# One core, two layers of FFN, mixer and FFN: products on the raw residual, LayerNorm applied when they leave PSUM

## The chip, the core and the metric

The kernel runs on one core of a Trainium2 chip, in one launch. The metric is the time on the device in microseconds. A core has TensorE (PE) for matmuls, VectorE (DVE) and ScalarE (ACT) for elementwise work, GpSimd (POOL), and DMA queues, here all fed by SyncE (SP). The engines run side by side, each through its own list of instructions in order, and wait for each other by semaphores.

## What is computed

Two layers over 384 tokens, 128 of context and 256 latent, of width 1024. Each layer is a gated FFN, a mixer (latent attention beside a bidirectional RG-LRU behind one input projection) and a second gated FFN. Each sub-layer's input is the normalised residual, scaled and shifted by modulation vectors that differ between the two kinds of token:

```
def trunk_layer(x, mod, mixer, lp):
    m = [mod[:, k, None, :] for k in range(N_MOD)]
    h = x * (1 + m[1]) + m[0]
    x = layer_norm(ALPHA * x + 0.5 * m[2] * swiglu(h, lp["w_ffn_up"][0], lp["w_ffn_down"][0]),
                   lp["ln_g"][0], lp["ln_b"][0])
    h = x * (1 + m[4]) + m[3]
    y, aux = mixer(h)
    x = layer_norm(ALPHA * x + m[5] * y, lp["ln_g"][1], lp["ln_b"][1])
    h = x * (1 + m[7]) + m[6]
    x = layer_norm(ALPHA * x + 0.5 * m[8] * swiglu(h, lp["w_ffn_up"][1], lp["w_ffn_down"][1]),
                   lp["ln_g"][2], lp["ln_b"][2])
    return x, aux

def swiglu(h, w_up, w_down):
    u = jnp.einsum("btd,df->btf", h, w_up)
    return jnp.einsum("btf,fd->btd", jax.nn.silu(u[..., :D_FF]) * u[..., D_FF:], w_down)
```

The modulation is silu(cond) @ w_mod + b_mod, nine vectors of 1024 per layer. D_FF is 2816.

## The kernel before

The residual X lies in SBUF with features on the partitions, as KD = 8 chunks of 128 features by T = 384 tokens; COND are the two token ranges, 0 to 128 and 128 to 384. Every product runs as three matmuls: weights and inputs are each split into a high and a low part, and `mm3` (lines 319 to 322) adds wh·xh, wh·xl and wl·xh. `piece` (line 306) makes the weight parts: ScalarE casts wh (line 315), VectorE subtracts for wl (line 316), both put ahead in the order by a priority. Three buffers hold split weights, four PSUM tiles hold accumulators. `hh` and `hl` are the two parts of a sub-layer's input. A scheduler lays the instructions of each engine in one order at build time, so what stands behind a waiting instruction waits too.

An FFN (`ffn`, line 466) has 22 pairs of products, gate and value, each of 8 chunks, so 48 matmuls a pair. `gated` (line 472) takes a pair out of PSUM: silu on ScalarE, a product on VectorE (line 475), a cast on ScalarE, a subtraction on VectorE (line 477). The down products follow, and `Residual.add` (line 347) adds each finished chunk into X (line 351). GpSimd sums X and its squares over the chunks (lines 360 and 361).

At each of the five boundaries between sub-layers `next_input` (line 453) runs: some modulation steps, then `boundary_vectors`, then `moments` (line 378: mean and deviation per token, by small matmuls against a constant), then `normalise` (line 394), which subtracts the mean and multiplies by the reciprocal deviation chunk by chunk on VectorE (lines 400 and 401), out of PSUM tiles in which both are broadcast over the partitions. `split_affine` (line 275) turns each chunk into hh and hl: on ScalarE, with VectorE taking half of the chunks' h (line 284) and all subtractions (line 286). GpSimd scales X for the residual (line 461). Products of the next sub-layer can start when the first chunk is through.

The mixer (line 536) projects with 14 products: four for the convolution and the RG-LRU (`conv` reads PSUM directly), two for the KV latent, one for the rotary key, three for the query, four for the gate branch. GpSimd turns the rotary key's weights (lines 608 and 609) and takes the power for the KV norm (line 335). The output product w_o goes two columns blocks at a time, one after the other.

Between all this `Pump` makes the modulation vectors from 18 MB of weights each layer, a step at a time: a step of `by_vector` is eight VectorE instructions of 512 columns (lines 250 and 252), a step of `by_tensor` goes over TensorE (line 238). The tables say where:

```
PUMPED = (by_vector((0, 2), (0, 3), (0, 4)) + by_tensor((0, 5)) + by_tensor((0, 6), (0, 7)) + by_tensor((0, 8), (1, 0))
          + by_vector((1, 1), (1, 3), (1, 4)) + by_tensor((1, 2)) + by_tensor((1, 5), (1, 6)) + by_tensor((1, 7), (1, 8)))
UP = [f for f in range(3, 21) if f % 3]
PLAN = ((UP, ()), (UP, ()), ((), ()), ((), ()))
NEXT_STEPS = (3, 3, 4, 3, 3)
MIX_STEPS = (14, 10)
```

So there are twelve vector steps in FFN (0,0) and twelve in FFN (0,1), three or four tensor steps at each boundary, 14 and 10 in the mixers.

## Time and profile before

| | |
|---|---|
| median of 3 runs | 1605.43 us (1602.26 to 1608.64) |
| the profiled execution | 1607.12 us, of which the profile's span is 1605.3 us |
| busy share of the span | PE 97%, DVE 59%, ACT 41%, POOL 10% |
| matmul instructions | 9234 |
| end of FFN (0,0) and start of mixer 0 | 315 us |
| mixer 0 to FFN (0,1) | 510 to 545 us |
| FFN (0,1) to FFN (1,0) | 809 to 832 us |
| FFN (1,0) to mixer 1 | 1096 us |
| mixer 1 to FFN (1,1) | 1294 to 1325 us |

Times in the rows are microseconds from the span's start. An engine's busy time is the sum of its instructions' records; a matmul's record is longer than the distance to the next one's start, because they are pipelined. "<-" behind a row's idle time names what released the engine. In names, a number behind the tile is left out.

### The profile page before, as it was taken

How to read it: one execution, taken by the hardware profiler on the slowest of the kernel's cores; microseconds unless marked ns; L12 is line 12 of the kernel's file. 1: busy time of each engine (PE TensorE's matmuls, PEld its weight loads, DVE VectorE, ACT ScalarE, POOL GpSimd, SP SyncE). 2: the span in 40 equal slices, each digit the busy share in tenths (PEclk: the TensorE clock that was granted, in tenths of full speed). 3: DMA queues.
4: the chain of work that ended last, by engine and by line, in shares of the span. 5: the costliest groups of instructions: out<-in, count | busy, mean ns of one | idle time of the engine just before them, and what ended most of it. 6: DMA issues, size and time to landing. Idle time of an engine off the chain costs nothing.

```text
span 1605.3 us, 22927 instructions
## 1 busy us (share of the span) xinstructions
PE 1552.4 (97%) x9234; PEld 1448.7 (90%) x9234; DVE 949.3 (59%) x1568; ACT 660.5 (41%) x1068; POOL 161.0 (10%) x142
## 2 busy tenths in 40 slices
PE   6999999999999999999999999999999989999997
PEld 5899999987668899999989999997867789999996
DVE  3778754477986946863474444345788664444334
ACT  3533323268743533332253333234775444333321
POOL 0000002220004100001220000032000240000011
PEclk9999999999999999999999999999999989999998
DMA  8866563346644535563454343334565214433331
GB/s 295 278 215 203 173 202 133 116 151 209 226 166 157 184 117 199 184 203 119 134 183 150 106 137 119 128 107 157 152 193 197 79 53 131 142 121 128 121 118 40
DMA packets 214790, 249.93 MB, mean 156 GB/s; under 512 B 26394, under 2 KB 193308, under 8 KB 211612
## 3 DMA queue, kind: packets, MB, share of 16 engines
q1 hardware_dynamic: 214684, 248.47, 46.6%
q8 instruction: 72, 1.18, 0.3%
q14 instruction: 34, 0.28, 0.1%
HBM read 245.52 MB, written 1.88 MB: 154 GB/s over the span
## 4 chain that ended last, share of the span: by engine, by line
PE 87%; DVE 5%; issue 3%; DMA 2%; ACT 2%; POOL 1%; SPq 0%; DVEq 0%; POOLq 0%; ACTq 0%
PE acc L320 26%; PE acc L321 26%; PE acc L322 26%; PE gm L238 2%; DVE wl L316 1%; PE acc L753 1%; DMA wm<-in_w_mod_dram 1%; PE ms L375 1%; PE pv L786 1%; DMA ws<-in_w_ffn_up_dram 1%; PE ms L769 1%; ACT wh L315 0%; DVE hl L286 0%; POOL sum_f L361 0%; PE ms L320 0%
## 5 line engine op out<-in xcount | busy, mean ns | idle before, releaser
L315 ACT CAST wh<-ws 128x1024 fp32r<-128x1024 f32 (+1 forms) x332 | 336.2, 1014 | 779.4 <-PE acc L321 545.3
L316 DVE TENSOR_TENSOR wl<-ws,wh 128x1024 fp32r<-128x1024 f32 (+1 forms) x332 | 411.3, 1240 | 382.3 <-ACT wh L315 380.7
L320 PE MATMUL acc<-hh,wh 128*128 128x384 f32 x1280 | 428.6, 339 | 7.9 <-ACT hh L278 7.4
L322 PE MATMUL acc<-hh,wl 128*128 128x384 f32 x1280 | 431.0, 337 | 2.9 <-DVE wl L316 2.9
L321 PE MATMUL acc<-hl,wh 128*128 128x384 f32 x1280 | 431.1, 338 | 1.1 <-DVE hl L286 1.0
L320 PEld LDWEIGHTS acc<-hh,wh 128*128 128x128 f32 x1280 | 241.8, 190 | 15.7 <-ACT hh L278 9.2
L322 PEld LDWEIGHTS acc<-hh,wl 128*128 128x128 f32 x1280 | 241.9, 189 | 8.6 <-DVE wl L316 5.5
L321 PEld LDWEIGHTS acc<-hl,wh 128*128 128x128 f32 x1280 | 241.9, 189 | 8.5 <-DVE hl L286 4.9
L320 PE MATMUL acc<-gh,wh 128*128 128x384 f32 x704 | 236.9, 336 | 0.0
L321 PE MATMUL acc<-gl,wh 128*128 128x384 f32 x704 | 236.4, 336 | 0.0
L322 PE MATMUL acc<-gh,wl 128*128 128x384 f32 x704 | 236.1, 335 | 0.0
L320 PEld LDWEIGHTS acc<-gh,wh 128*128 128x128 f32 x704 | 132.2, 188 | 0.4 <-issue 0.4
L321 PEld LDWEIGHTS acc<-gl,wh 128*128 128x128 f32 x704 | 132.4, 188 | 0.0
L322 PEld LDWEIGHTS acc<-gh,wl 128*128 128x128 f32 x704 | 132.2, 188 | 0.0
L475 DVE TENSOR_TENSOR a<-a,acc 128x384 f32<-128x384 f32 x87 | 48.1, 553 | 123.1 <-PE acc L322 121.4
L252 DVE SCALAR_TENSOR_TENSOR gsum<-wm,sil,gsum 128x512 f32<-128x512 f32 x168 | 120.2, 764 | 0.0
L320 PE MATMUL acc<-hh_in,wh 128*128 128x384 f32 x336 | 111.6, 337 | 5.9 <-ACT hh_in L278 5.9
L321 PE MATMUL acc<-hl_in,wh 128*128 128x384 f32 x336 | 113.9, 339 | 0.0
L322 PE MATMUL acc<-hh_in,wl 128*128 128x384 f32 x336 | 113.9, 339 | 0.0
L360 POOL TENSOR_TENSOR sum_f<-X 128x384 f32<-128x384 f32 x4 | 5.1, 1281 | 841.2 <-DVE X L351 841.2
L320 PEld LDWEIGHTS acc<-hh_in,wh 128*128 128x128 f32 x336 | 62.7, 188 | 7.8 <-ACT hh_in L278 6.8
L238 PE MATMUL gm<-wm,sil 128*32 128x128 f32 (+2 forms) x640 | 62.2, 428 | 3.3 <-DVE G L915 1.2
(268 smaller groups left out, 1750.4 us busy)
## 6 DMA issues: line engine op xcount, KB each, us to landing
ws<-in_w_ffn_up_dram SPq DMA_DIRECT2D x84, 1024.0 KB, 5.1
wm<-in_w_mod_dram SPq DMA_DIRECT2D x56, 1024.0 KB, 6.6
ws<-in_w_ffn_down_dram SPq DMA_DIRECT2D x32, 1024.0 KB, 5.3
wm<-in_w_mod_dram SPq DMA_DIRECT2D x32, 512.0 KB, 4.5
ws<-in_w_ffn_down_dram SPq DMA_DIRECT2D x16, 768.0 KB, 4.5
ws<-in_w_in_dram SPq DMA_DIRECT2D x12, 1024.0 KB, 5.3
...
```

Source lines behind the costliest of these rows:

```text
L238: nc.tensor.matmul(self.ps[32 * g : 32 * g + 32, :n], lhsT, wv[:, g], start=self.fresh, stop=stop)
L252: nc.vector.scalar_tensor_tensor(self.sum[:, r], wv[:, kk], s, self.sum[:, r], op0=ALU.mult, op1=ALU.add)
L315: nc.scalar.copy(parts[0], src)
L316: nc.vector.tensor_tensor(parts[1], src, parts[0].bitcast(F32), op=ALU.subtract)
L320: nc.tensor.matmul(ps, wh, xh, start=start, stop=False)
L321: nc.tensor.matmul(ps, wh, xl, start=False, stop=False)
L322: nc.tensor.matmul(ps, wl, xh, start=False, stop=stop)
L375: nc.tensor.matmul(self.pt[:, 2 * i + j : 2 * i + j + 1], src[:, i * P : (i + 1) * P], mean_w[:, 0:1], start=False, stop=stop and i == T / ...
L475: nc.vector.tensor_tensor(a, a, px[:, :T], op=ALU.mult)
L753: nc.tensor.matmul(views[i], qT[hf][0:96, h % 4, q0 : q0 + P], kT[hf][0:96, h % 4, k0:k1], start=True, stop=True)
L769: nc.tensor.transpose(t0[:, (2 * j + i) * P : (2 * j + i + 1) * P], pr_[:, (0, 512)[i] + j * P : (0, 512)[i] + (j + 1) * P], ident)
L786: nc.tensor.matmul(o[:, P:T], v, pTs[e][:, (j - 1) * 256 : j * 256], start=(j == 1), stop=(j == 3))
```

## The change

The new `hh` and `hl` are wider: EXT = T + 4 columns. In the first 384 columns of chunk c stands G·X, with G = (1 + scale)·ln_g per feature and kind of token, split into high and low part by `split_raw` as soon as X of that chunk is final; nothing of the mean is taken off. `extend` puts -G of the two kinds of token and then B of both (B = (1 + scale)·ln_b + shift) into the four extra columns. A product over all 388 columns gives W·G·X, -W·G and W·B. `settle` takes it out of PSUM: it copies the four columns, adds mean · (-W·G) to the product by token range, and multiplies by the reciprocal deviation; the last two columns are handed on as a bias. `stats` (the small matmuls and the power) and `broadcasts` (mean and deviation over all partitions, copied by ScalarE to SBUF as stat tiles) run between the first products of the next sub-layer. `carry` then brings X itself to its normalised and scaled form on GpSimd, three instructions a chunk, where VectorE did two and GpSimd one before.

In the mixer all 14 products go through `settled`, and their readers take the bias in separate instructions for the two token ranges; conv's first product is held until mean and deviation are there. In w_o the last two blocks run together over the chunks, and the other chunks are split before their residuals are added. The step tables move: the boundaries have none, the mixers 20 and 16, FFN (0,1) four, and FFN (1,0) twelve, four of them on TensorE and eight on VectorE.

```diff
-          + by_vector((1, 1), (1, 3), (1, 4)) + by_tensor((1, 2)) + by_tensor((1, 5), (1, 6)) + by_tensor((1, 7), (1, 8)))
+          + by_vector((1, 1)) + by_tensor((1, 2)) + by_vector((1, 3), (1, 4)) + by_tensor((1, 5), (1, 6)) + by_tensor((1, 7), (1, 8)))
-PLAN = ((UP, ()), (UP, ()), ((), ()), ((), ()))
-NEXT_STEPS = (3, 3, 4, 3, 3)
-MIX_STEPS = (14, 10)
+PLAN = ((UP, ()), (UP[:4], ()), (UP, ()), ((), ()))
+MIX_STEPS = (20, 16)
+EXT = T + 4
...
+    def split_raw(c, G):
+        h32 = tmp.tile([P, T], F32, tag="t1", bufs=3, name=f"raw_{n_ps[0]}_{c}")
+        for r, (t0, t1) in enumerate(COND):
+            nc.scalar.activation(hh[:, c, t0:t1], X[:, c, t0:t1], AF.Copy, scale=G[:, c, r : r + 1])
+            nc.vector.tensor_scalar_mul(h32[:, t0:t1], X[:, c, t0:t1], G[:, c, r : r + 1])
+        nc.vector.tensor_tensor(hl[:, c, :T], h32, hh[:, c, :T].bitcast(F32), op=ALU.subtract)
...
+        def extend(self):
+            for o, v, sign in ((T, self.G, -1.0), (T + 2, self.B, 1.0)):
+                nc.scalar.mul(hh[:, :, o : o + 2], v, sign)
+                nc.vector.scalar_tensor_tensor(hl[:, :, o : o + 2], v, sign, hh[:, :, o : o + 2].bitcast(F32),
+                                               op0=ALU.mult, op1=ALU.subtract)
+        def broadcasts(self):
...
+            self.mean, self.rstd = (tmp.tile([P, T], F32, tag=f"sum{i}", name=f"stat{i}_{name}", bufs=1) for i in range(2))
+            nc.scalar.copy(self.mean, pm[:, :T])
+            nc.scalar.copy(self.rstd, pr[:, :T])
+        def carry(self):
             for c in range(KD):
-                nc.vector.tensor_tensor(X[:, c, :], X[:, c, :], pm[:, :T], op=ALU.subtract)
-                nc.vector.tensor_tensor(X[:, c, :], X[:, c, :], pr[:, :T], op=ALU.mult)
-                yield c
+                nc.gpsimd.tensor_tensor(X[:, c, :], X[:, c, :], self.mean, op=ALU.subtract)
+                nc.gpsimd.tensor_tensor(X[:, c, :], X[:, c, :], self.rstd, op=ALU.mult)
+                nc.gpsimd.tensor_scalar(X[:, c, :], X[:, c, :], self.ag[:, 0, c : c + 1], self.ag[:, 1, c : c + 1],
+                                        op0=ALU.mult, op1=ALU.add)
+        def settle(self, dst, ps, name):
+            v = tmp.tile([P, 4], F32, tag="ext", name=f"ext_{name}")
+            nc.vector.tensor_copy(v, ps[:, T:EXT])
+            for r, (t0, t1) in enumerate(COND):
+                nc.vector.scalar_tensor_tensor(dst[:, t0:t1], self.mean[:, t0:t1], v[:, r : r + 1], ps[:, t0:t1],
+                                               op0=ALU.mult, op1=ALU.add)
+            nc.vector.tensor_tensor(dst, dst, self.rstd, op=ALU.mult)
+            return v[:, 2:4]
...
-    def next_input(res, l, s, nl, nm, steps):
-        pump.step(steps)
-        pump.finish()
-        G, B, ag = boundary_vectors(l, s, nl, nm)
-        hh, hl = h_tiles(f"{nl}{nm}")
-        for c in res.normalise():
-            split_affine(hh, hl, c, G, B)
-        for c in range(KD):
-            nc.gpsimd.tensor_scalar(X[:, c, :], X[:, c, :], ag[:, 0, c : c + 1], ag[:, 1, c : c + 1],
-                                    op0=ALU.mult, op1=ALU.add)
-        return hh, hl
...
+                    bg = raw.settle(a, pg, f"g{l}{s}{f}")
+                    by = raw.settle(y, px, f"y{l}{s}{f}")
+                    for r, (t0, t1) in enumerate(COND):
+                        nc.scalar.activation(a[:, t0:t1], a[:, t0:t1], AF.Silu, bias=bg[:, r : r + 1])
+                        nc.vector.scalar_tensor_tensor(a[:, t0:t1], y[:, t0:t1], by[:, r : r + 1], a[:, t0:t1],
+                                                       op0=ALU.add, op1=ALU.mult)
...
-                    product(pg[:, :T], wg, i * P, hh, hl)
-                    product(px[:, :T], wx, i * P, hh, hl)
-                    gated(f, pg, px)
+                    product(pg, wg, i * P, width)
+                    if prev is not None and f == 0:
+                        prev.stats()
+                    product(px, wx, i * P, width)
+                    if prev is not None and f == 0:
+                        prev.broadcasts()
+                    gated(f, pg, px, prev)
+                    if prev is not None and f == 0:
+                        prev.carry()
```

What this does to the order on the engines, at three places. First VectorE (DVE) at the boundary from FFN (0,0) to mixer 0; `wl` are low parts of weights, `h` and `hl` the input, `ms` the broadcast mean and deviation, `m_f` the variance. Before:

```order
L351 SCALAR_TENSOR_TENSOR X<-acc_2655,gate_2125,X 128x128
L351 SCALAR_TENSOR_TENSOR X<-acc_2655,gate_2125,X 128x256
L316 TENSOR_TENSOR wl_3072<-ws_3068,wh_3071 128x1024
L400 TENSOR_TENSOR X<-X,ms_2832 128x384
L389 SCALAR_TENSOR_TENSOR m_f_2883<-ms_2824,m_f_2883 128x3
L400 TENSOR_TENSOR X<-X,ms_2832 128x384 x5
L401 TENSOR_TENSOR X<-X,ms_2888 128x384 x2
L284 TENSOR_SCALAR h_66_0_2894<-X,G_2866,B_2867 128x128
L284 TENSOR_SCALAR h_66_0_2894<-X,G_2866,B_2867 128x256
L401 TENSOR_TENSOR X<-X,ms_2888 128x384
L286 TENSOR_TENSOR hl_2875<-h_66_0_2894,hh_2874 128x384
```

and in the changed kernel, where `raw_7` is chunk 7 times G and `ext` the four columns:

```order
L360 SCALAR_TENSOR_TENSOR X<-acc_2696,gate_2122,X 128x128
L360 SCALAR_TENSOR_TENSOR X<-acc_2696,gate_2122,X 128x256
L291 TENSOR_SCALAR raw_7_2873<-X,G_2124 128x128
L291 TENSOR_SCALAR raw_7_2873<-X,G_2124 128x256
L322 TENSOR_TENSOR wl_3040<-ws_3036,wh_3039 128x1024
L292 TENSOR_TENSOR hl<-raw_7_2873,hh 128x384
L429 COPY ext_0ux_3007<-acc_2918 128x4
L322 TENSOR_TENSOR wl_3084<-ws_3036,wh_3083 128x1024
L394 SCALAR_TENSOR_TENSOR m_f_2961<-ms_2947,m_f_2961 128x3
L429 COPY ext_0ux_3022<-acc_2966 128x4
L322 TENSOR_TENSOR wl_3164<-ws_3160,wh_3163 128x1024
L431 SCALAR_TENSOR_TENSOR s0ux_3006<-stat_f_3002,ext_0ux_3007,acc_2918 128x128
```

The sixteen instructions over all chunks are gone; behind the last addition to X stand five instructions to the input's last part, with one weight split among them, and the first settle stands behind the third split.

Second VectorE in the up products of FFN (1,0), about pairs 15 and 16 before and 17 after; `gsum` are the modulation steps, `gl` the low part of the gated product. Before:

```order
L475 TENSOR_TENSOR a_15_8363<-a_15_8363,acc_8306 128x384
L316 TENSOR_TENSOR wl_8438<-ws_8368,wh_8437 128x1024
L477 TENSOR_TENSOR gl_7327<-a_15_8363,gh_7326 128x384
L316 TENSOR_TENSOR wl_8466<-ws_8370,wh_8465 128x1024
L475 TENSOR_TENSOR a_16_8430<-a_16_8430,acc_8373 128x384
```

and after:

```order
L433 TENSOR_TENSOR a_17_9072<-a_17_9072,stat_f_7599 128x384
L431 SCALAR_TENSOR_TENSOR y_17_9073<-stat_f_7598,ext_y_9079,acc_9015 128x256
L252 SCALAR_TENSOR_TENSOR gsum_9005<-wm_4_8825,sil,gsum_9005 128x512
L433 TENSOR_TENSOR y_17_9073<-y_17_9073,stat_f_7599 128x384
L252 SCALAR_TENSOR_TENSOR gsum_9005<-wm_4_8825,sil,gsum_9005 128x512
L506 SCALAR_TENSOR_TENSOR a_17_9072<-y_17_9073,ext_y_9079,a_17_9072 128x128
L506 SCALAR_TENSOR_TENSOR a_17_9072<-y_17_9073,ext_y_9079,a_17_9072 128x256
L252 SCALAR_TENSOR_TENSOR gsum_9005<-wm_4_8825,sil,gsum_9005 128x512
L509 TENSOR_TENSOR gl_7505<-a_17_9072,gh_7504 128x384
L252 SCALAR_TENSOR_TENSOR gsum_9005<-wm_4_8825,sil,gsum_9005 128x512 x4
L322 TENSOR_TENSOR wl_9222<-ws_9102,wh_9221 128x1024
```

A weight split now stands behind the settles of a pair and up to seven or eight additions of a modulation step.

Third GpSimd (POOL) at the start of mixer 0; `r_f` is the reciprocal deviation, `ws` the rotary key's weights, `r_kv` the KV norm's power. Before:

```order
L391 TENSOR_TENSOR r_f_2886<-m_f_2883,mhalf 128x3
L461 TENSOR_SCALAR X<-X,ag_2868 128x384 x8
L608 COPY ws_3321<-ws_3321 128x8x16
L609 COPY ws_3321<-ws_3321 128x8x16
L335 TENSOR_TENSOR r_kv_3301<-v_kv_3299,mhalf 128x3
```

and the end of the 24 carry instructions after:

```order
L421 TENSOR_TENSOR X<-X,stat_f_3002 128x384
L423 TENSOR_SCALAR X<-X,ag_2126 128x384
L422 TENSOR_TENSOR X<-X,stat_f_3003 128x384
L673 COPY ws_3343<-ws_3343 128x8x16
L423 TENSOR_SCALAR X<-X,ag_2126 128x384
L674 COPY ws_3343<-ws_3343 128x8x16
L341 TENSOR_TENSOR r_kv_3323<-v_kv_3321,mhalf 128x3
```

The weights' copies and the power stand behind 23 and 24 carry instructions where 8 scalings stood before.

## Rows read from the trace of the kernel before

**Rows 1.** The page, chain that ended last: shares of the span by engine.
```profile
PE 87%; DVE 5%; issue 3%; DMA 2%; ACT 2%; POOL 1%; SPq 0%; DVEq 0%; POOLq 0%; ACTq 0%
```

**Rows 2.** Timeline of PE, matmuls of 384 and 512 columns: start, length, instruction.
```profile
559.84 0.33 PE L322 MATMUL acc<-hh,wl 128*128 128x384 f32 x1
...
560.36 0.34 PE L322 MATMUL acc<-hh,wl 128*128 128x384 f32 x1
...
403.23 0.40 PE L320 MATMUL acc<-ckh,wh 128*128 128x512 f32 x1
...
403.70 0.39 PE L322 MATMUL acc<-ckh,wl 128*128 128x512 f32 x1
```

**Rows 3.** Windows at FFN starts: stretch, length, PE PEld DVE ACT busy; acc, ms, gm.
```profile
510.27:545.00 34.73, 21.16 (x102) 18.49 (x102) 0.74 (x2) 0.63 (x2) 0.95 0.29 97
809.00:832.00 23.00, 11.44 (x62) 10.59 (x63) 0.74 (x2) 0.00 (x0) 1.00 0.61 229
1294.19:1325.00 30.81, 19.45 (x92) 17.81 (x91) 0.74 (x2) 0.00 (x0) 0.83 0.10 35
...
sum 88.54, PE 17.37 PEld 13.84 DVE 24.85 ACT 0.52; mean PE 5.79 PEld 4.61 DVE 8.28 ACT 0.17
...
sum 88.54, PE 8.29 PEld 2.84 DVE 1.64; mean PE 2.76 PEld 0.95 DVE 0.55
```

**Rows 4.** Windows, all engines (PE PEld DVE ACT POOL busy): two mixers, two FFNs.
```profile
315.30:431.00 115.70, 111.49 (x659) 91.41 (x659) 92.36 (x180) 81.97 (x141) 15.24 (x18) 0.99 0.58 190
1096.16:1215.20 119.04, 113.09 (x626) 91.27 (x627) 91.65 (x172) 82.03 (x142) 14.69 (x18) 0.97 0.57 188
549.30:710.50 161.20, 161.20 (x978) 159.41 (x977) 111.86 (x163) 55.11 (x76) 0.00 (x0) 1.00 0.56 187
840.40:998.50 158.10, 158.10 (x914) 158.10 (x913) 65.99 (x78) 55.20 (x76) 0.00 (x0) 1.00 0.40 132
```

**Rows 5.** Lines on DVE: count, busy us, mean ns | idle before, releaser.
```profile
L316 DVE TENSOR_TENSOR wl<-ws,wh 128x1024 fp32r<-128x1024 f32 (+1 forms) x332 | 411.3, 1240 | 382.3 <-ACT wh L315 380.7 <-issue 0.4
L252 DVE SCALAR_TENSOR_TENSOR gsum<-wm,sil,gsum 128x512 f32<-128x512 f32 x168 | 120.2, 764 | 0.0
L477 DVE TENSOR_TENSOR gl<-a,gh 128x384 fp32r<-128x384 f32 x88 | 48.5, 551 | 0.6 <-ACT gh L476 0.6
L286 DVE TENSOR_TENSOR hl<-h,hh 128x384 fp32r<-128x384 f32 x40 | 26.4, 659 | 4.7 <-ACT h L281 4.6
L351 DVE SCALAR_TENSOR_TENSOR X<-acc,gate,X 128x128 f32<-128x128 f32 x64 | 23.8, 413 | 31.0 <-PE acc L322 29.7
L284 DVE TENSOR_SCALAR h<-X,G,B 128x128 f32<-128x128 f32 (+1 forms) x40 | 15.2, 420 | 0.0
L231 DVE TENSOR_TENSOR modv<-gmt,small 128x8 f32<-128x8 f32 (+2 forms) x30 | 4.9, 163 | 0.4
```

**Rows 6.** Timeline of DVE, packed stretch of FFN (0,1).
```profile
642.79 2.73 DVE L252 SCALAR_TENSOR_TENSOR gsum<-wm,sil,gsum 128x512 f32<-128x512 f32 x4
645.44 1.22 DVE L316 TENSOR_TENSOR wl<-ws,wh 128x1024 fp32r<-128x1024 f32 x1
646.58 2.07 DVE L252 SCALAR_TENSOR_TENSOR gsum<-wm,sil,gsum 128x512 f32<-128x512 f32 x3
```

**Rows 7.** Timelines of POOL and DVE around the start of FFN (1,0).
```profile
806.79 1.02 POOL L360 TENSOR_TENSOR sum_f<-sum_f,X 128x384 f32<-128x384 f32 x1 [16.79 <-DVE X L351]
...
819.30 0.66 POOL L461 TENSOR_SCALAR X<-X,ag 128x384 f32<-128x384 f32 x1 [4.05 <-DVE h L284]
...
824.47 1.46 POOL L461 TENSOR_SCALAR X<-X,ag 128x384 f32<-128x384 f32 x1 [0.21 <-ACT hh L278]
...
806.81 2.08 DVE L316 TENSOR_TENSOR wl<-ws,wh 128x1024 fp32r<-128x1024 f32 x1 [0.17 <-ACT wh L315]
```

**Rows 8.** Timeline of POOL in mixer 0: weights' copy and the KV norm's power.
```profile
345.24 0.29 POOL L608 COPY ws<-ws 128x128 f32<-128x128 f32 x1 [7.40 <-DVE uc L817]
...
374.20 1.77 POOL L335 TENSOR_TENSOR r_kv<-v_kv,mhalf 128x3 f32<-128x3 f32 x1 [28.44 <-DVE v_kv L333]
```

More of the change, by code (lines that the diff above doesn't have):

```diff
@@ L341, in hybrid_step_kernel, with __init__ @@
         broadcast = True
-        def __init__(self, name, gate):
+        early = True
+        def __init__(self, name, gate, after=None):
             self.name, self.gate = name, gate
+            if after is not None:
+                self.G, self.B, self.ag = boundary_vectors(*after)
             self.sums = [tmp.tile([P, T], F32, tag=f"sum{i}", name=f"sum{i}_{name}", bufs=1) for i in range(2)]
@@ L352, in add @@
                                                    op0=ALU.mult, op1=ALU.add)
+                if last and self.broadcast:
+                    split_raw(c, self.G)
                 sq = self.sums[1]
@@ L356, in add @@
                 nc.scalar.activation(sq, X[:, c, :], AF.Square)
+            if c < KD - 1 and self.early:
+                split_raw(c, self.G)
             if c == 0:
@@ new lines, in stats @@
+            nc.tensor.matmul(self.pt[:, :6], mean_w, zeros, start=True, stop=False)
+            for src, stop in ((self.sums, False), (self.tail, True)):
+                for j in range(2):
+                    self.columns(j, src[j], stop=stop and j == 1)
+            mv = self.pt[:, :6].rearrange("p (a b) -> p a b", b=2)
+            m2 = tmp.tile([P, 4], F32, tag="m2", name=f"m2_{name}")
+            nc.scalar.activation(m2[:, :3], mv[:, :, 0], AF.Square)
+            nc.vector.scalar_tensor_tensor(m2[:, :3], mv[:, :, 1], LN_EPS, m2[:, :3], op0=ALU.add, op1=ALU.subtract)
@@ L404, in hybrid_step_kernel, with __init__ @@
     class LastResidual(Residual):
         broadcast = False
-        def __init__(self, name, gate):
+        early = False
+        def __init__(self, name, gate, after=None):
             super().__init__(name, gate)
@@ L500, in ffn @@
             nc.vector.tensor_scalar_mul(gate, modv[l][:, m], 0.5)
[L501 removed]
+            res = (Residual if after else LastResidual)(f"f{l}{s}", gate, after)
             for j in range(KD // 2):
@@ L534, in token_scale, with mixer @@
         return pr
-    def mixer(l, hh, hl, steps):
+    def mixer(l, prev, steps, after):
         w_in = A["w_in"][l]
@@ L556, in mixer, with settled, convolved @@
             gw = load_gates(l)
+            prev.extend()
+            def settled(ps, name):
+                u = tmp.tile([P, T], F32, tag="t1", bufs=3, name=f"s{l}{name}")
+                b = prev.settle(u, ps, f"{l}{name}")
+                return u, [(t0, t1, b[:, r : r + 1]) for r, (t0, t1) in enumerate(COND)]
+            def convolved(c, ps):
+                u, parts = settled(ps, f"ux{c}")
+                for t0, t1, b in parts:
+                    nc.scalar.activation(u[:, t0:t1], u[:, t0:t1], AF.Identity, bias=b)
+                conv(l, c, us[c], u)
+            held = None
             for c in range(NLC):
@@ L560, in mixer @@
                 ps = acc_tile()
-                product(ps[:, :T], w, (c % 2) * P, hh, hl)
-                conv(l, c, us[c], ps)
+                product(ps, w, (c % 2) * P, EXT)
+                if c == 0:
+                    prev.stats()
+                    held = ps
+                elif c == 1:
+                    prev.broadcasts()
+                    convolved(0, held)
+                if c > 0:
+                    convolved(c, ps)
+            prev.carry()
             lru = lru_steps(l, lp, gw, us)
@@ L936, in hybrid_step_kernel @@
     lam = vec["lam"]
-    sp_t = [const.tile([P, 16], F32, name=f"spt{i}") for i in range(4)]
-    na, ee, s1, s2 = sp_t
+    sp_t = tmp.tile([P, P], F32, tag="nat", name="spt")
+    na, ee, s1, s2 = (sp_t[:, 16 * i : 16 * (i + 1)] for i in range(4))
     nc.vector.tensor_scalar_mul(na, lam, -1.0)
```

172 lines of the change are left out of this document (89 added, 83 removed).

## The prediction

> **What bounds the kernel now.** I read the chain of waits first. TensorE work is 87% of it and VectorE 5% [rows 1]. So a change helps only where TensorE stands still, and hurts where it adds matmul columns or makes VectorE the later engine. Next come the two matmul spacings. Three products of 384 columns start within 0.52 us, that is 0.173 us each; two of 512 columns within 0.47 us, 0.235 each [rows 2]. The records give each matmul about 0.34 us because neighbours overlap, so a busy sum hides small gaps; I count matmuls times spacing instead.
>
> The third reading is of the three stretches in which an FFN takes over from the layer ahead of it, from the end of the residual's products to a steady stream. They last 88.54 us. Their 102, 62 and 92 products fill 256 x 0.173 = 44.3 us; the small matmuls of statistics and of modulation are busy for 17.37 and 8.29 us [rows 3]. That leaves 88.5 - 70.0 = 18.5 us idle, and more if the small matmuls overlap in their records as the big ones do; if two thirds of their time is real, 27. I take 21. The two mixers' projection stages, whose starts are the other two boundaries, show 115.70 - 111.49 = 4.2 and 119.04 - 113.09 = 5.95 us without a TensorE record [rows 4]. Together at least 29 us of the span is TensorE waiting at boundaries, at most about 37.
>
> VectorE is the engine to watch: in the steady FFN stretch with modulation steps it is busy 111.86 of 161.20 us, without them 65.99 of 158.10, and in the mixers 92.36 of 115.70 and 91.65 of 119.04 [rows 4]. GpSimd has next to nothing there.
>
> **The change, part by part.**
>
> *The boundary wait goes.* Products start on the residual's chunks as they fall due, so subtraction of the mean, multiplication, affine step and the 3 to 4 modulation steps no longer stand ahead of them. Gain: 21 + 8 = 29 us (8 of the mixers' 10, since some of that idle time lies later in the stage). What is late next is the last chunk. For a boundary behind an FFN, chunk 7 needs two residual additions (0.41 each), two scalings (0.42 each), one weight split queued between (1.24) and a subtraction (0.55) [rows 5]: 3.5 us, against 21 matmuls on chunks 0 to 6, 3.6 us. About 0.5 us stays, three times. Behind a mixer, chunks 6 and 7 end together: both chains, 0.8 + 0.8 + 0.8 + 0.8 + 1.2 + 0.55 + 0.55 = 5.5 us, with 18 matmuls (3.1 us) as cover, and some hand-over; 3 us stays, twice. Together **+7.5**.
>
> *Four more columns.* (0.235 - 0.173) / 128 is 0.48 ns a column, 1.9 ns for four. They are in 3 FFNs x 44 products and 2 mixers x 14, each of 24 matmuls: 3,840 matmuls, **+7.4 us**, all on the path.
>
> *Settling in the FFNs.* For one pair of products VectorE gains two settles: a four-column copy (0.16), two multiply-adds out of PSUM (2 x 0.41), a product (0.55), 1.53 us each, and two multiply-adds where one product stood (0.82 for 0.55). By durations VectorE then needs 2 x 1.24 + 3.06 + 0.82 + 0.55 = 6.9 us. But packed instructions start sooner than their durations say: a split of 1.22 us is followed after 1.14, four modulation additions take 2.65 [rows 6]. At 0.08 less for each of 13 instructions it is 5.9 us, under TensorE's 48 x 0.175 = 8.4. So settling alone costs nothing; TensorE hides it.
>
> *Steps in FFN (1,0).* Eight vector steps (64 additions) now stand in that FFN beside the settling, between pairs 6 and 21. VectorE: 16 x 5.9 + 64 x 0.66 + some 2 for transposes = 138 us; by durations 16 x 6.9 + 64 x 0.764 = 159 [rows 5]. TensorE: 16 x 8.4 = 134. VectorE is the later by 4 to 25, less a lead of some 6 us that the four accumulators and three split buffers give. The order shows the weight splits queued behind the additions, so TensorE waits when the lead is gone. Packed rows are nearer to what will happen than means: **+4** (0 to 19). FFN (0,1) loses most of its steps, but TensorE was never short there [rows 4], so this gives nothing.
>
> *The residual on GpSimd.* Each boundary puts 16 additions-like instructions (1.02 alone) and 8 scalings (0.66 alone) [rows 7] on GpSimd: 21.6 us, against 5.3 before, under the first three pairs. Nobody needs X until the residual is added, much later; cover is complete on that side. The cost is what VectorE loses. A split of 1.22 us [rows 6] took 2.08 beside a GpSimd addition, and a GpSimd scaling of 0.66 took 1.46 while VectorE worked [rows 7]: either loses, by 0 to 0.86 us. In three pairs some 21 VectorE instructions read two SBUF operands; at half, 0.43, that is 9 us against 3 x (8.4 - 5.9) = 7.5 of slack. I take 1 us for each of the three FFNs, **+3** (0 to 24).
>
> The nearest rows thus show a mean loss well under a whole instruction. The Trainium skill, page "SBUF — State Buffer", section "SBUF: two separate sides", says that VectorE and GpSimd share a port pair by an exclusive lock: whichever starts first holds it for its whole instruction and the other stands still. Here the wait in rows 7 agrees, 0.86 us of 1.02; that VectorE loses every time is not shown.
>
> *Settling in the mixers.* VectorE loses 16 normalising instructions (0.55 each, as a product of their size) and seven or eight splits of the input (0.66, with two scalings of 0.42 in half of them), about 16 us [rows 5], and gains 14 settles of 1.2 to 1.5, 17 to 21. About 24 of its instructions meet the carry: +10 at 0.43. 92 + 4 + 10 = 106 us. It also can't settle before mean and deviation are out, two products and the statistics in (about 13 us), where only four splits can run: some 8 us lost. That makes 114, about the 112 to 116 that TensorE then needs. On GpSimd the copies of the rotary key's weights and the power of the KV norm stand behind 22 to 24 carry instructions; before, they ran at 30 and 59 us into the stage [rows 8]. The carry starts about 13 us in and lasts 22 to 33, so it ends 35 to 46 us in: after the first of these times, before the second. I take **+5** a mixer (0 to 20), +10.
>
> *Tail.* The last residual's statistics are no longer begun early: 6 more small matmuls in the chain, **+1**.
>
> Sum: -29 + 7.5 + 7.4 + 4 + 3 + 10 + 1 = +3.9 us. The profiled execution took 1607.1 us (its span 1605.3 and 1.8 around it), so its counterpart is 1611. It stands 1.7 above the median of the runs, 1605.4, and so the median to expect is **1609**.
>
> **The rivals.**
>
> *VectorE keeps up everywhere* (chance 0.31). The mixers' extra work fits into the 23 and 27 us that VectorE has free there, and the collisions and the late steps are eaten by slack. For it: packed starts, accumulators ahead by two pairs. Against it: 106 of 114 us leaves little. Then -29 + 7.5 + 7.4 + 1 = -13, 1592; with all 37 us of idle time gone, 1584.
>
> *VectorE becomes the mixers' bound* (0.15). One mechanism: conv and gates are VectorE's own long chain, they can't begin before the first settle, and each GpSimd instruction that gets in first delays them further, with the KV norm's power behind the carry. It decides from the point where VectorE's 106 us and the lost start exceed TensorE's stage: at 0.86 a collision instead of 0.43 it is 124, and waits of TensorE in the order's fixed sequence come on top. +20 for each mixer instead of 5: 1609 + 30 = 1639.
>
> *The carry stops VectorE for its whole length* (0.09). Each boundary costs VectorE 21.6 us. An FFN has 7.5 of slack and 6 of lead, so 8 come through, three times, 21 more than my 3; the mixers lose 11 to 12 more each: +44, 1653. It is the page's rule with GpSimd always first; row 824.47 speaks against it, where GpSimd was the one that waited [rows 7].
>
> *The wait stays under another name* (0.05). Chunk 7's scaling or the weights' splits come late in VectorE's queue, and half of the 29 us remains: 1609 + 14 = 1623.
>
> **How the numbers follow.** My forecast, 1600 to 1618, has 0.40. A measurement of this kernel can tell about 0.5%, 8 us, from no change: below 1597.4 is faster, above 1613.4 slower. The forecast gives 0.03 faster, 0.26 same, 0.11 slower; the first rival 0.27 faster and 0.04 same; the other three 0.29 slower. Together 0.30, 0.30, 0.40. The range 1586 to 1640 leaves out the carry's rival (0.09), the upper third of the mixers' (0.05) and the lowest end of the first (0.05).
>
> **What would show it.** In the changed kernel's trace: no gap over 1 us at the start of FFN and mixer streams behind an FFN, about 3 us behind a mixer; 388-column matmuls 0.175 us apart; in FFN (1,0) from pair 12 on TensorE waiting for the weights' split or VectorE's settles, 4 us in all; splits of 1.3 to 2.1 us under the carry; in the mixers VectorE over 90% busy, with TensorE's waits on settles and on the rotary key's weights of some 5 us. I am wrong if the 388-column matmuls cost more than 2 ns extra, if the mixers' stages end as early as TensorE's matmuls allow, or if GpSimd's carry needs much more than 33 us.

## The result: slower by 4%, and the profile after

The changed kernel takes 1669.26 us (median, 1668.5 to 1673.27) against 1607.04 for the kernel before on the same chip: a ratio of 1.0397 (1.0366 to 1.0427). The forecast, 1609 with 1586 to 1640, was wrong: the end of the carry's rival, 1653, was the farthest it reached. The profiled execution has a span of 1671.5 us. Its page: the busy rows, and TensorE's granted clock in 40 slices (tenths of the full clock, 9 for 0.9 or more).

```profile
PE 1583.8 (95%) x9234; PEld 1480.1 (89%) x9234; DVE 1186.0 (71%) x2252; ACT 687.1 (41%) x1156; POOL 254.5 (15%) x222
...
PEclk9999999989999899999998999999899999999998
```

VectorE works 237 us more than before, GpSimd 94; TensorE 31, with the same number of matmuls. What TensorE waits for, in sum over the span (line, releaser: us, times, longest):

```profile
PE acc L328 <- DVE wl L322: 21.9, 6, 8.6
PE ms L327 <- DVE ucl L928: 10.5, 2, 5.3
PE ms L326 <- ACT kr L639: 6.4, 2, 3.2
...
PE acc L326 <- DVE qT L792: 5.4, 6, 2.0
PE acc L327 <- DVE hl L292: 4.0, 7, 1.4
```

The first three, 38.8 us, are waits that the kernel before did not have at that size. The table gives the stages of the profiled executions, from the timelines of TensorE: a mixer's ends where attention's first product with the values (tile pv) starts, an FFN's where its down products start. The columns on the right are experiments told below. The kernel before was run beside each of them, with medians from 1606.5 to 1608.2 us, so a comparison across experiments is uncertain by some 2 us from this alone.

| stage, us | before | changed | e1_ag | e2_nocarry | e9_bare | e10_hybrid |
|---|---|---|---|---|---|---|
| mixer 0, projections to attention | 127.9 | 144.6 | 142.9 | 133.6 | 132.3 | 129.8 |
| attention, w_o, FFN (0,1) up | 273.5 | 288.8 | 281.2 | 279.0 | 275.8 | 269.1 |
| FFN (1,0) up | 195.5 | 212.7 | 202.4 | 199.8 | 198.1 | 202.3 |
| mixer 1, projections to attention | 131.3 | 147.8 | 146.0 | 133.0 | 133.6 | 128.5 |
| attention, w_o, FFN (1,1) up | 267.9 | 266.1 | 264.7 | 270.6 | 263.0 | 263.6 |

Each of the first four loses 15 to 17 us, as if from one cause. It is two causes in the FFNs and another in the mixers.

### The profile page after: what moved, and what is told of

It is laid out like the page before. It is cut to its first block, busy times and chain, and to the rows that moved or that the text cites. A ratio compares the mean times of both kernels' runs of the same rounds, so it can differ in the third digit from the quotient of the medians.

```text
span 1671.5 us, 23746 instructions
## 1 busy us (share of the span) xinstructions
PE 1583.8 (95%) x9234; PEld 1480.1 (89%) x9234; DVE 1186.0 (71%) x2252; ACT 687.1 (41%) x1156; POOL 254.5 (15%) x222
## 5 line engine op out<-in xcount | busy, mean ns | idle before, releaser
L328 PE MATMUL acc<-hh,wl 128*128 128x388 f32 (+1 forms) x1744 | 600.9, 345 | 21.2 <-DVE wl L322 21.2
L326 PE MATMUL acc<-hh,wh 128*128 128x388 f32 (+1 forms) x1744 | 600.6, 345 | 9.1 <-ACT hh L276 5.9
L327 PE MATMUL acc<-hl,wh 128*128 128x388 f32 (+1 forms) x1744 | 601.9, 345 | 4.0 <-DVE hl L292 4.0
L328 PEld LDWEIGHTS acc<-hh,wl 128*128 128x128 f32 x1744 | 334.5, 192 | 27.9 <-DVE wl L322 23.9
L326 PEld LDWEIGHTS acc<-hh,wh 128*128 128x128 f32 x1744 | 334.0, 192 | 16.0 <-ACT hh L276 6.8
L327 PEld LDWEIGHTS acc<-hl,wh 128*128 128x128 f32 x1744 | 335.4, 192 | 10.2 <-DVE hl L292 6.3
L327 PEld LDWEIGHTS acc<-gl,wh 128*128 128x128 f32 x704 | 132.3, 188 | 0.0
L508 ACT CAST gh<-a 128x384 fp32r<-128x384 f32 x88 | 45.0, 512 | 165.2 <-DVE a L506 162.1
L505 ACT ACTIVATE a<-a,ext_g 128x128 f32<-128x128 f32 (+1 forms) x132 | 53.2, 449 | 114.4 <-DVE a L433 74.6
L509 DVE TENSOR_TENSOR gl<-a,gh 128x384 fp32r<-128x384 f32 x88 | 49.4, 561 | 26.9 <-ACT gh L508 26.9
L506 DVE SCALAR_TENSOR_TENSOR a<-y,ext_y,a 128x128 f32<-128x128 f32 (+1 forms) x132 | 55.2, 460 | 2.2
```

What stands on the lines that cost most here:

```text
L326: nc.tensor.matmul(ps, wh, xh, start=start, stop=False)
L327: nc.tensor.matmul(ps, wh, xl, start=False, stop=False)
L328: nc.tensor.matmul(ps, wl, xh, start=False, stop=stop)
L505: nc.scalar.activation(a[:, t0:t1], a[:, t0:t1], AF.Silu, bias=bg[:, r : r + 1])
L506: nc.vector.scalar_tensor_tensor(a[:, t0:t1], y[:, t0:t1], by[:, r : r + 1], a[:, t0:t1], op0=ALU.add, op1=ALU.mult)
L508: nc.scalar.copy(gh[:, f, :], a)
```

## Experiment 1: a buffer that VectorE waited for

In FFN (0,1), stretches of 10 us (length, busy of PE, PEld, DVE, ACT, POOL, clock, DMA), then single instructions of VectorE, GpSimd and TensorE, then VectorE's waits for this in sum:

```profile
560.00:570.00 10.00, 10.00 (x58) 10.00 (x57) 5.70 (x9) 3.72 (x7) 10.00 (x10) 1.00 0.01 2
570.00:580.00 10.00, 5.18 (x30) 4.86 (x28) 0.00 (x0) 0.00 (x0) 10.00 (x13) 1.00 0.00 0
580.00:590.00 10.00, 6.18 (x27) 6.19 (x28) 7.18 (x18) 2.77 (x5) 1.41 (x2) 0.66 0.38 123
...
565.28 0.55 DVE L433 TENSOR_TENSOR a<-a,stat_m 128x384 f32<-128x384 f32 x1
581.54 0.17 DVE L484 TENSOR_SCALAR ag<-small 128x8 f32<-128x8 f32 x1 [15.71 <-POOL X L423]
...
580.85 0.67 POOL L423 TENSOR_SCALAR X<-X,ag 128x384 f32<-128x384 f32 x1
...
583.82 0.69 PE L328 MATMUL acc<-hh,wl 128*128 128x388 f32 x1 [8.64 <-DVE wl L322]
...
DVE ag L484 <- POOL X L423: 29.3, 2, 15.7
```

From 565.8 to 581.5 VectorE does nothing and hardly any data is loaded; ScalarE ends its last instruction at 567.6, and TensorE runs on to 575.2 with what was ready. GpSimd works all the time. VectorE's next instruction writes 0.17 us worth of `ag`, the scale and shift of X for a boundary to come. `ag` has two buffers, and five are written in all: this is the fourth, for the boundary behind FFN (1,0), whose carry starts at 1164 us, and not the next boundary's, as the expectation below has it. The buffer that it gets is read by the carry under way, and falls free with the carry's last instruction. The scheduler has put that write between the two settles of pair 1, since nothing but the buffer holds it:

```
L433 TENSOR_TENSOR a_1_5093<-a_1_5093,stat_m_4990 128x384
L484 TENSOR_SCALAR ag_9460<-small_621 128x8
L485 TENSOR_SCALAR ag_9460<-small_621 128x8
L429 COPY ext_y_5100<-acc_5036 128x4
```

So settles and weight splits stand behind a wait for all 24 carry instructions; TensorE uses up its lead, stands 8.64 us, and then has a clock of 0.66 for a while. FFN (1,0) has the same, 13.6 us for VectorE and 8.5 for TensorE.

```diff
-        ag = tmp.tile([P, 2, KD], F32, tag="ag", name=f"ag{l}{s}")
+        ag = tmp.tile([P, 2, KD], F32, tag="ag", name=f"ag{l}{s}", bufs=5)
```

> Five buffers for the tile ag instead of two; nothing else. Theory A (a wait on a buffer): in the changed kernel VectorE stood still 15.7 and 13.6 us in FFN (0,1) and FFN (1,0), at the write of the next boundary's ag, until GpSimd's last carry instruction released the buffer; TensorE lost 8.6 and 8.5 us of it and some 2 to 4 us each at a lower clock after it. Then this kernel is 20 to 26 us below the changed one (1669 to about 1645), with no TensorE gap over 1 us in these two places, and the mixers unchanged. Rival B (the carry itself holds VectorE by the port): VectorE stands still for another reason as long as the carry runs, and the time falls by under 8 us.

1653.38 us, 15.9 below the changed kernel; ratio to before 1.0286 (1.0268 to 1.0303). The same stretches now:

```profile
560.00:570.00 10.00, 10.00 (x58) 10.00 (x57) 8.95 (x14) 3.84 (x7) 10.00 (x9) 1.00 0.01 2
570.00:580.00 10.00, 10.00 (x58) 10.00 (x58) 8.29 (x13) 3.21 (x5) 10.00 (x10) 1.00 0.61 199
580.00:590.00 10.00, 10.00 (x59) 10.00 (x58) 8.29 (x14) 3.20 (x5) 7.82 (x6) 1.00 0.04 12
```

TensorE is busy throughout, and VectorE works beside the carry. Theory A holds, short of its size: a semaphore it was, not the port. The two FFN stages fell by 7.6 and 10.3 us. The three added buffers also move the tiles that lie behind them: the down products of FFN (0,1) stand 0.1734 us apart in the changed kernel and 0.1767 here, which for 528 matmuls is 1.7 us. So the wait alone is worth some 17.6 us (an estimate), still under the 20 to 26 expected.

## Experiments 2 and 5: the carry beside VectorE

The edit of e2 is `for c in range(0)` in `carry`.

> As e1_ag, but the carry is left out: X is not normalised between sub-layers, so this is no longer the reference's computation. It prices GpSimd's work beside VectorE. Theory A: VectorE's convolution instructions in the mixers took 0.75 us under the carry against 0.41 alone, which holds up the RG-LRU's products (5.3 us on ucl) and the rotary key's copy (3.2 us on kr), twice; without the carry the mixers' projection stages fall by 8 to 12 us each with the clock loss behind the gaps, FFNs by 0 to 2, together 16 to 26 below e1_ag. Rival: the mixers wait because settling comes late (no settle before mean and deviation), not because of GpSimd; then less than 8 us.

1630.56 us, 22.8 below e1_ag. Mixer 0 fell by 9.3 us, mixer 1 by 13.0, FFN (0,1) and (1,0) by 2.2 and 2.6; FFN (1,1) rose by 5.9. So the carry costs 22 us in the mixers. The convolution's multiply-adds on VectorE show how: under the carry in the changed kernel, then in e2 (twelve instructions in each row), then the waits of TensorE that they led to in the changed kernel.

```profile
334.35 8.95 DVE L902 SCALAR_TENSOR_TENSOR uc<-s0ux,small,uc 128x126 f32<-128x126 f32 x12 [0.33 <-ACT uc L897]
...
337.10 4.02 DVE L902 SCALAR_TENSOR_TENSOR uc<-s0ux,small,uc 128x126 f32<-128x126 f32 x12 [0.62 <-ACT uc L897]
...
347.80 0.47 PE L326 MATMUL ms<-uch,wh 128*128 128x384 f32 x1 [3.20 <-ACT kr L639]
...
356.21 0.69 PE L327 MATMUL ms<-ucl,wh 128*128 128x384 f32 x1 [5.28 <-DVE ucl L928]
```

0.75 us each against 0.34: in the chain that the RG-LRU waits for, an instruction loses 0.4 us on average. TensorE's wait on kr has the same root: ScalarE's copy of the cached key (L639) stands behind the bias of a settled chunk, which had waited 5.85 us for VectorE. Before the change conv read its input from PSUM; now it reads the settled copy in SBUF, so these instructions have two SBUF operands. That this decides is seen in FFN (0,1) of the changed kernel, where the carry ends at 581.5 us:

```profile
560.84 2.08 DVE L506 SCALAR_TENSOR_TENSOR a<-y,ext_y,a 128x128 f32<-128x128 f32 x2
563.02 0.74 DVE L431 SCALAR_TENSOR_TENSOR a<-stat_m,ext_g,acc 128x128 f32<-128x128 f32 x2
...
581.89 0.74 DVE L431 SCALAR_TENSOR_TENSOR y<-stat_m,ext_y,acc 128x128 f32<-128x128 f32 x2
584.26 0.75 DVE L506 SCALAR_TENSOR_TENSOR a<-y,ext_y,a 128x128 f32<-128x128 f32 x2
```

The settles' multiply-adds (L431), which read the product in PSUM, take 0.74 us for two beside the carry and after it; those with all tensors in SBUF (L506) take 2.08 and 0.75. The Trainium skill's lock ("SBUF — State Buffer", section "SBUF: two separate sides") names just such instructions, VectorE's with two SBUF inputs beside a GpSimd instruction that reads SBUF. In the convolution the loss is 0.4 us on average beside GpSimd instructions of 0.9 to 1.2, as if the two engines took turns, and not a VectorE that stands still for the carry's length.

Would a later carry avoid this?

```diff
+            nc.vector.scalar_tensor_tensor(prev.mean, rr, 0.0, prev.mean, op0=ALU.mult, op1=ALU.add)
+            prev.carry()
```

> As e1_ag, but in the mixers the carry starts only behind the query norm (mean is rewritten there by one VectorE instruction that adds 0 times rr, and the carry reads it), so that GpSimd is free while convolution, RG-LRU and rotary key go through VectorE. Leaving the carry out gave 9 us in mixer 0 and 13 in mixer 1. Theory: it is GpSimd beside the convolution's chain that costs; late, it meets instructions that read PSUM, and each mixer falls by 6 to 12 us, the kernel by 12 to 24 to some 1632 to 1641. Rival: the collisions only move to keys, queries and gates, and the mixers fall by under 4 us each.

1648.95 us (runs from 1645.6 to 1652.8), 4.4 below e1_ag (1651.2 to 1654.4); mixer 0 at 139.7 (3.2 less), mixer 1 at 145.2 (0.8 less). The rival holds. TensorE's waits for the convolution fell, in sum of both mixers, to the second row, but it now waits at the queries:

```profile
PE acc L326 <- DVE qT L793: 14.9, 4, 7.3
PE ms L327 <- DVE ucl L929: 2.8, 2, 1.5
```

This was the only other place that was tried; whether the mixer has one where VectorE has nothing urgent stays open.

## Experiments 3, 6, 7 and 13: what a matmul costs

> As e1_ag, but all products run over 384 columns, and settle copies four columns of the product itself, so the result is not the reference's. The input tiles keep their pitch of 388. It prices the four columns: the changed kernel's matmuls stood 0.1767 us apart in steady stretches against 0.1733 before, 3.3 ns, where the prediction had 1.9. If the columns cost it, the spacing returns to 0.1733 and the time falls by 12 to 13 us against e1_ag; at 1.9 ns by 7; if it is the pitch of 388 that slows the reads, the spacing stays above 0.175 and the time falls by under 4.

1645.9 us (two runs), 7.5 below e1_ag, but the spacing did not come back. The windows that count the accumulators' matmuls in 100 us of a steady up phase, 1400 to 1500, for before, changed kernel, e3_width, e6_pitch388, e13_shift and e9_bare, in this order:

```profile
1400.00:1500.00 100.00, 100.00 (x579) 100.00 (x578) 6.64 (x12) 5.78 (x12) 1.00 0.40 132
...
1400.00:1500.00 100.00, 100.00 (x568) 100.00 (x567) 21.47 (x72) 0.00 (x0) 1.00 0.39 127
...
1400.00:1500.00 100.00, 100.00 (x571) 99.90 (x570) 22.41 (x75) 0.00 (x0) 1.00 0.39 127
...
1400.00:1500.00 100.00, 100.00 (x571) 99.87 (x570) 6.65 (x12) 5.31 (x11) 1.00 0.37 122
...
1400.00:1500.00 100.00, 100.00 (x571) 100.00 (x570) 6.65 (x12) 5.79 (x12) 1.00 0.38 124
...
1400.00:1500.00 100.00, 100.00 (x578) 100.00 (x578) 21.52 (x72) 0.00 (x0) 1.00 0.38 124
```

579 in the kernel before, 568 in the changed one, 571 with 384 columns read from tiles that are 388 wide. By starts over long rows that is 0.1733, 0.1767 and 0.1756 us: the four columns are worth 1 ns, which for 3,840 matmuls is 4 of the 7.5 us, the rest being open, and 2.3 ns come from something else. The next run is the kernel before with wider tiles and nothing else.

```diff
-        hh = act.tile([P, KD, T], F32R, tag="hh", name=f"hh_{name}")
-        hl = act.tile([P, KD, T], F32R, tag="hl", name=f"hl_{name}")
+        hh = act.tile([P, KD, T + 4], F32R, tag="hh", name=f"hh_{name}")[:, :, :T]
+        hl = act.tile([P, KD, T + 4], F32R, tag="hl", name=f"hl_{name}")[:, :, :T]
```

> The kernel before, with nothing changed but that each chunk of hh and hl takes 388 columns in SBUF, of which 384 are used. With 384 columns on a pitch of 388 the matmuls of e3_width still stood 0.1758 us apart against 0.1733 before. If the pitch (chunks that begin at 1552 bytes each) does it, the up products' matmuls here stand 0.1758 apart and the kernel is some 10 to 12 us slower than before (4 FFNs x 1056 and 2 mixers x 576 matmuls at 2.4 ns are 13 us, less where TensorE waits). Rival: it is something else in the changed kernel (settling, its reads of PSUM); then spacing and time are those of before.

1621.51 us, ratio 1.0094 (1.0067 to 1.012), and 571 matmuls in 100 us: the same loss without any of the change.

> As e1_ag, but hh's chunks lie 400 columns (1600 bytes) apart, hl's still 388 (to make room, the tile nat has one buffer; the opening may lose 1 to 2 us). If a pitch that is no multiple of 64 bytes slows the reading, the two of three matmuls that read hh start their successor 2.4 ns sooner and only those with hl stay: mean spacing 0.1767 to about 0.1751, some 6 us less. Rival: any pitch but 384 costs the same, or it is no matter of the pitch: spacing stays 0.1767.

1650.79 us (two runs), 2.6 below e1_ag, and 0.1763 us a matmul: a pitch of 64 bytes' multiples for hh is not the repair.

> The kernel before, with 128 bytes of padding behind hh, so that hl begins 128 bytes later; pitch 384, nothing else. In e11_behind_mixers FFN (1,0) read both with a pitch of 384 and still ran at 0.1755 us a matmul, where hl began 12416 bytes behind hh instead of 12288. If the start of hl does it, this kernel's up products run at 0.1755 too and it is 8 to 13 us slower than before; if it is not the start, 0.1733 and no change.

```diff
+        hh = act.tile([P, KD * T + 32], F32R, tag="hh", name=f"hh_{name}")[:, : KD * T].rearrange("p (k t) -> p k t", k=KD)
```

1622.9 us, ratio 1.0091 (1.0063 to 1.012), 571 matmuls again. Padding of 128 bytes behind hh, no other pitch, costs the kernel before some 15 us. All tiles behind hh move with hl, the split weights too, so it is shown that where tiles start in SBUF sets TensorE's pace here. The trace of e13 points at hl: its matmuls with hl start 0.1813 us after the one before, the two others 0.1704 and 0.1751, where in the kernel before all three stand 0.1734 to 0.1736 apart; and the down products, whose split weights moved as well, keep 0.1733. That it is hl alone is not shown, and which addresses are good stays open: the slower pace sometimes also went on into the down products, which read other tiles (0.1767 us in FFN (0,1) of e1_ag, 0.1735 in FFN (1,0) of the same run).

## Experiments 4 and 8: the statistics and the clock

The mean granted clock is 0.974 in the changed kernel, 0.986 before; with 1584 and 1552 us of busy TensorE that is at most some 41 against 22 us of time lost to it. This is an estimate from above, since part of the low clock falls into waits and behind the last product; within TensorE's records it is 31 against 16. One place is behind each boundary; the kernel before has it behind four of the five. In the changed kernel 24 one-column matmuls stand in a row of 2.9 us behind the first product, and this is what follows in mixer 0, a fall to the lower of the clock's two levels, 1.2 of 2.4 GHz (stretches of 1 us, columns as above):

```profile
322.00:323.00 1.00, 1.00 (x11) 1.00 (x11) 0.91 (x1) 0.00 (x0) 0.00 (x0) 1.00 0.00 0
323.00:324.00 1.00, 1.00 (x8) 1.00 (x8) 0.16 (x1) 0.17 (x1) 0.26 (x1) 1.00 0.01 1
324.00:325.00 1.00, 1.00 (x6) 1.00 (x5) 0.00 (x0) 0.00 (x0) 0.62 (x1) 0.59 0.80 202
325.00:326.00 1.00, 1.00 (x5) 1.00 (x4) 0.00 (x0) 0.00 (x0) 0.00 (x0) 0.50 0.69 191
```

> As e1_ag, but the statistics over the first seven chunks are started when chunk 6 is added, as in the kernel before, not between the first products of the next sub-layer. In the changed kernel 24 one-column matmuls ran in one row of 2.9 us behind each boundary's first product, and for 3 to 4 us behind it TensorE's granted clock was 0.5. Theory: a row half as long costs less or no clock; 1 to 2 us for each of five boundaries, 5 to 10 us below e1_ag behind the FFNs above all. Rival: the clock falls all the same, since the other half still runs in a row, or TensorE now waits for GpSimd's sums of chunk 6: no gain, or some us slower.

1659.83 us, 6.5 above e1_ag. Behind the FFNs the clock no longer falls after the row, now of 12 matmuls and 1.4 us, but TensorE now waits up to 5.7 us for GpSimd's sum of chunk 6 behind the mixers, where both last chunks end together.

> As e1_ag, but the statistics' one-column matmuls of a boundary stand two by two between the matmuls of the second product instead of in one row ahead of it. Theory: the granted clock of 0.5 for 3 to 4 us behind each boundary comes from the row of 2.9 us in which TensorE does little; spread out, the clock stays at 1.0 there and 1.7 us are gained five times, 6 to 9 us in all. Rival: the clock falls for another reason (the wait on the last chunk's hl), and nothing changes, or settling comes later by the second product's length and costs some us.

1655.8 us, no gain. The windows behind the boundary to FFN (1,0) in e1_ag, the same in e8_spread, and in e8_spread behind mixer 0:

```profile
842.00:846.00 4.00, 4.00 (x17) 4.00 (x17) 0.16 (x1) 0.17 (x1) 0.86 (x1) 0.57 1.00 319
...
845.00:850.00 5.00, 5.00 (x37) 5.00 (x36) 1.01 (x2) 0.17 (x1) 0.00 (x0) 1.00 0.96 324
850.00:855.00 5.00, 5.00 (x29) 4.47 (x28) 3.38 (x9) 2.48 (x5) 3.03 (x3) 1.00 0.09 29
...
545.00:550.00 5.00, 4.43 (x17) 4.44 (x18) 2.66 (x5) 0.55 (x3) 0.18 (x1) 0.59 0.42 135
550.00:555.00 5.00, 5.00 (x21) 5.00 (x21) 1.39 (x2) 1.01 (x1) 0.00 (x0) 0.50 0.52 170
```

Behind the three FFNs the clock stays at 1.00 once the small matmuls are spread, as expected; 3.4 us at half the clock would be worth 1.7 us each. It does not always fall with the row either: in the profiles of the seven kernels that have it behind all three FFNs (changed, e1, e2, e3, e5, e7, e9) it fell behind 17 of 21 such boundaries, in e4 and e8 behind none of three each. Behind the mixers it falls all the same, and longer, since TensorE also waits there for the last chunks. What is won at one boundary is lost at another; what the clock would be without these waits stays open.

## Experiments 9 to 12: what is left, and where it pays

> The changed kernel with its own ag buffers (e1_ag), without the carry, without the four columns and with a pitch of 384: X is not normalised, settle copies columns of the product itself, so this is not the reference's computation. What is left of the change is products on the raw input, settling, the order of the steps. Theory (the costs add up: buffer 16, carry 23, columns and pitch 15 to 17): e1_ag's 1653 less 23 less 16 is some 1614, still 5 to 10 above before, so that the boundaries' gain (13 us of recorded idle time) is eaten by settling and by the lower clock. Rival: columns and carry overlap, and 1620 or more is left; or the boundaries did gain what was forecast and it falls to 1600 or below.

1615.87 us, ratio 1.0051 (1.0034 to 1.0067): 14.7 below e2_nocarry, with matmuls at 0.1733 us. So the changed kernel's 62.6 us over before (1606.7 in this series) are 15.9 for the buffer, 22.8 for the carry, 14.7 for columns and addresses, and 9.2 for the rest: settling in the mixers and the clock, less what the boundaries win. No run separates these three. The mean granted clock is 0.979 here against 0.986, which on its own would be some 11 us (an estimate from the two spans).

> As e1_ag for the three FFNs, but the mixers take their input as before: mean and deviation applied on VectorE out of PSUM, GpSimd scaling X, products of 384 columns, no settling and no carry in them. Steps and pitch stay as in e1_ag. Theory: the two mixers' stages (142.9 and 146.0 us in e1_ag, 127.9 and 131.3 before) come back to 129 to 133, so 1653 falls to 1623 to 1630; what stays above before is columns and pitch in the FFNs (3 x 3.5) and pitch in the mixers (2 x 1 to 2), w_o and settling. Rival: the loss is in the FFNs as much, and it stays above 1635.

1616.06 us, ratio 1.006 (1.0035 to 1.0086). Taking the raw input out of the two mixers alone is worth 37.3 of the 46 us by which e1_ag is slower. Better than the theory; the FFNs behind the mixers are now 4.4 and 4.3 us below before (the next expectation puts the first at 5.6).

So a version with the raw input behind the mixers only should win. e11 does that, with one buffer seen at two pitches:

```diff
+    flat = [act.tile([P, KD * EXT], F32R, name=n) for n in ("hh", "hl")]
+    hh, hl = (t[:, : KD * T].rearrange("p (k t) -> p k t", k=KD) for t in flat)
+    eh, el = (t.rearrange("p (k t) -> p k t", k=KD) for t in flat)
```

> Products on the raw input only where it paid in e10_hybrid, in the two FFNs behind the mixers (their stages with w_o fell by 5.6 and 4.3 us against before); mixers and FFN (1,0) take their input as before, statistics included. hh and hl are one flat buffer each, seen with a pitch of 388 in those two FFNs and of 384 everywhere else, so only 2112 matmuls pay for pitch and columns. Steps: boundaries into mixers and FFN (1,0) 3, 4 and 3, mixers 17 and 13, FFN (0,1) four on VectorE, FFN (1,0) eight. Theory: mixers and FFN (1,0) as before to 2 us, the two FFNs 4 to 6 below each, the kernel 6 to 11 below before, some 1596 to 1601. Rival: what the two FFNs win is lost where the steps go (mixers 17 and 13), or by a lower clock elsewhere; then within 4 us of before.

1629.4 us, ratio 1.0153 (1.0125 to 1.0181). A new wait, of TensorE at the statistics behind each mixer:

```profile
528.80 0.37 PE L388 MATMUL ms<-mean_w,sum_m 128*128 128x1 f32 x1 [7.97 <-POOL sum_m L376]
...
1321.04 0.37 PE L388 MATMUL ms<-mean_w,sum_m 128*128 128x1 f32 x1 [3.37 <-POOL sum_m L376]
```

Chunks of the two views overlap, so the raw splits wait until w_o has read the buffer. These waits are 11.3 of the 22.5 us; FFN (1,0) is 9 us longer than before, with matmuls 0.1756 us apart, and what else it lost stays open.

> As e11_behind_mixers, with two repairs: w_o and what it reads also use the pitch of 388, so that the raw splits of the first chunks need not wait for the end of w_o (in e11 TensorE waited 8.0 and 3.4 us at the statistics because they did); and hh gets 128 bytes of padding, so that hl begins 12544 bytes behind it, a multiple of 256 as in the kernel before (tile nat has one buffer to make room). Theory: FFN (1,0) and the mixers go back to 0.1733 us a matmul and to the time of before, FFN (0,1) and (1,1) with w_o win 4 to 6 us each: 1596 to 1602. Rival: it is pitch and not start address that slows, and the steps moved to mixers and FFN (1,0) cost what the boundaries win: 1605 to 1612.

1615.49 us, ratio 1.0039 (1.0019 to 1.0059). Those waits are gone, and FFN (1,0) and the opening run at 0.1733 us; but FFN (0,1) with attention and w_o takes 281.2 us, 7.7 above before, while FFN (1,1) takes 263.5, 4.4 below. Behind mixer 0 the granted clock is 0.50 for 13.7 us there. FFN (1,0) and mixer 1, which took over modulation steps, are 5.0 and 3.4 us above before, as the rival said in kind. Nothing that was tried beats the kernel before.

## Why the forecast was wrong, step by step

The sum said +3.9 us, and +62.2 was measured. Most of the 58 us between lies in four terms, told below: a wait that the sum lacks (16 us), the carry in the mixers (their stages are 33 us longer instead of 10), the boundaries (worth 10 us instead of 21.5), and columns and tile addresses (15 us instead of 7). They overlap in part, so that they need not add up.

**The boundary wait: mis-sized.** Products do start at once. But the 29 us that I put down as waiting were not all waiting. My windows of [rows 3] show clocks of 0.95 and 0.83 beside the counts: 34.73 x 0.05 + 30.81 x 0.17 = up to 7 us of the 18.5 were products at a lower clock, which the changed kernel has too, and more of it. TensorE's records of all kinds in these three windows leave 88.54 - 76.66 = 11.9 us of waiting, where I took 21:

```profile
sum 88.54, PE 76.66 PEld 63.41 DVE 65.31 ACT 45.75 POOL 28.26; mean PE 25.55 PEld 21.14 DVE 21.77 ACT 15.25 POOL 9.42
```

With 2.0 us at the start of each mixer it is 16 us at five boundaries before, and 6 us in the changed kernel: 10 us won, where 29 - 7.5 = 21.5 were forecast. At the boundary to FFN (1,0) of before the waits are these:

```profile
809.80 0.83 PE L375 MATMUL ms<-mean_w,sum_f 128*128 128x1 f32 x6 [0.25 <-POOL sum_f L361]
819.15 0.79 PE L320 MATMUL acc<-hh,wh 128*128 128x384 f32 x3 [1.54 <-ACT hh L278]
820.42 0.44 PE L321 MATMUL acc<-hl,wh 128*128 128x384 f32 x1 [0.48 <-DVE hl L286]
```

2.3 us; the other 8 of that boundary were statistics and modulation steps, which only moved. **What stays**, 7.5 us, was about right: 6 us in all, 4.0 of them on hl.

**Four columns: wrong in size and cause.** 7.4 us forecast; 3,840 matmuls at 3.4 ns are 13, of which the columns are 1 ns and where the tiles lie the rest. The opening FFN, with no column more, pays 2 us of the same kind (1,056 matmuls at 0.1754 instead of 0.1734 us). Together that is about the 14.7 us of e9; runs e3, e6 and e13 show both parts. The rows that I took the price from compare two operand pairs of different tiles, which I did not notice.

**A missing step: the buffer.** I went through the order on VectorE for the boundary and for FFN (1,0), and passed by the two ag writes, since they cost 0.17 us. What I priced was their work, not what they wait for. That is 15.9 us (e1).

**The carry: the overlap in the mixers.** I took 5 us a mixer, with the range's end at 20. It is 9.3 and 13.0 for the carry alone. My count was right, 24 collisions at 0.43 us, 10 us a mixer: in mixer 0 of the changed kernel VectorE's instructions under the carry are 10.9 us longer than in e2, 7.7 of them in 22 multiply-adds of the convolution. So was the carry's place: it starts 16 us into the stage, lasts 27 and ends before the KV norm's power. What failed is what I set the 10 us against. I added them to VectorE's busy time, 106 or 114 of 112 to 116 us, and let the rest of the stage hide them. But conv leaves PSUM, so they all stand in one chain that TensorE waits for, 3.2 and 5.3 us in a mixer, with a low clock behind the waits. The rival with +20 each came nearest in its mechanism, with stages 16.7 and 16.5 us longer; without carry and columns (e9) 4.4 and 2.3 us of that are left. In two FFNs the carry costs 2 to 3 us each, where I had 1; FFN (1,1) was 5.9 us longer without it, which stays open.

**Settling and steps in FFN (1,0): right.** In e1_ag, without the buffer's wait, VectorE is busy 82.3 of 87.0 us between 950 and 1037 and TensorE all of it; TensorE waits 1.4 us for weight splits in this FFN, against my 4. **The tail** is 0.8 us longer in the changed kernel, forecast 1.

**The carry's rival**, +44 us by a lock held for 21 us a boundary, came nearest to the time, 1653 against 1669, by luck: VectorE did stand still for the carry, but for a semaphore, in two places, and elsewhere its instructions with two SBUF operands took some 0.4 us longer.
